# A third seven-product pair in the last step of both MLPs, totals added by accumulating transfers, main banks read out beside the last group

## The chip, the cores and the metric

The kernel runs on one core of one Trainium2 chip. The metric is the device time of one execution in microseconds (us); the time before is the median of three runs, 2081.15 us (2080.92 to 2085.08).

The core's engines are TensorE (PE in the profile, with its weight loads as PEld), VectorE (DVE), ScalarE (ACT), GpSimd (POOL) and SyncE (SP). SP issues the weight loads; POOL issues the transfers that add to their destination.

## The reference

Two layers over 256 tokens of width 2048. Layer 0 mixes with a gated short convolution, layer 1 with a stick-breaking attention; after each mixer comes a squared-ReLU MLP with a hidden width of 8192, and each sub-layer is added to the stream behind a norm. The change lies in the two MLPs only:

```python
def sq_relu_mlp(u, w_up, w_down):
    return jnp.square(jax.nn.relu(u @ w_up)) @ w_down

h = h + rmsnorm(sq_relu_mlp(u, mlp_w_up[i], mlp_w_down[i]), mlp_post_g[i])
```

## The kernel before

**Products.** Every fp32 operand is split into a high and a low part (`whi`, `wlo` for the weights), and a product is three matmuls: high by high, high by low, low by high. A weight chunk is 128 rows by 1024 columns. SP loads it into one of five buffers (`raw`, with the chunk's number behind it), ACT rounds it to `whi` (L184, or L233 in a seven), DVE subtracts to `wlo` (L195); seven buffers of each hold the parts. A `raw` buffer is given to the chunk five places later once both have read it, a `whi` and `wlo` buffer to the one seven places later once PE has used it.

**Eights and sevens.** A pair of chunks meets the two blocks of 128 tokens in eight products of 128 by 512 columns (24 matmuls, L1308 to L1310), or, by Winograd's scheme, in seven (21 matmuls). A seven costs DVE four differences of 128x512 over the weights (L225) and 3.5 splits in place of two, and four small differences of 128x128 over the hidden rows (L1170, with splits by L1127). Its parts carry the letters a, b, t, u and take four of the seven buffers. It needs four main banks in PSUM and four more for the products 1, 5, 6 and 7; combinations of these are then added to the main results.

**Steps.** Each MLP runs through eight steps e. In step e PE builds the hidden rows of step e+1 (`up`) and multiplies those of step e by the down weights. The last step (e = 7) has no `up`. It runs four pairs m = 0 to 3 onto the left half of the output, which close the main banks and the banks of the products 1, 5, 6 and 7, and then a last group of eight chunks onto the right half. Before the change m = 0 and 1 were sevens, m = 2 and 3 eights. Chunks 368 to 375 are the pairs and 376 to 383 the last group in MLP 0; 752 to 759 and 760 to 767 in MLP 1.

**The last group.** It reuses the banks of the products 1, 5, 6, 7 (numbers 6, 7, 0, 1), into which ACT first copies the partial results (L1375, `acc<-mg`). The blocks first take turns by units (a chunk against a block, both halves; 12 `acc` matmuls a chunk), over two chunks in MLP 1 and four in MLP 0; then each quarter of the output runs through its remaining chunks alone, so that its norm (`post`: a square on ACT, L687 or L779, and a gain on DVE, L567) starts as early as it can. Quarters are (block, column); (0,0) to (1,1) are the left half, (0,2) to (1,3) the right.

**Order.** PE keeps the order of the program. ACT and DVE are ordered when the kernel is built, by a scheduler with priorities (`tc.high_priority`), and while a norm runs, by a manual order that follows the program's own clock (`at(delay, fn)`, `spent(us)`). Each engine works through its rows in order, so a row that waits holds up all behind it. In MLP 0 the norm is followed by the groups for keys and values (`KeyNorms`, chunks from 384, banks 4, 5 for block 0 and 6, 7 for block 1), whose first operand is the transposed new residual; in MLP 1 by the output (`OutNorms`).

Of the kernel before, what the change touches and what calls it, by code (L numbers as in the profile page):

```python
# [14 lines left out]
P = 128  # L15
# [90 lines left out]
def trunk(ctx, tc, x, xT, vecs, rows, ws, out):  # L106
# [201 lines left out]
    def at(delay, fn):  # L308
        heappush(due, (clock["us"] + delay, clock["seq"], fn))
        clock["seq"] += 1  # L310

    def spent(us):
        clock["us"] += us
        while due and due[0][0] <= clock["us"]:
            heappop(due)[2]()
# [150 lines left out]
                self.add_total(r, ps, (b, c))  # L466
            self.then(b, c, r if not self.early else ps[:], r)

    def run(groups, enter=False, leave=None):

        units = [(gr, i) for gr in groups for i in range(gr.n)]
        first, last = EDGE if enter else 0, len(units) - (leave.edge if leave else 0)
# [645 lines left out]
    def mlp(pool, i, before, after):  # L1118
# [10 lines left out]
        class Hidden:  # L1129


            def __init__(self, e):
                self.xs, self.sums = [None] * (NF // 4), {}
# [7 lines left out]
            def tile(self, n, ps, half):  # L1141
                if n % 2 == 0:
                    held[n] = pool.tile([P, 2, T], F32, tag="s", name="s", bufs=2)
                both = held[n - n % 2]
                s = both[:, n % 2, :]
                with tc.high_priority():
                    nc.vector.tensor_tensor(s, ps[:, :T], half[:], op=ALU.add)  # L1147
                nc.scalar.activation(s, s, AF.Relu)  # L1148
                nc.scalar.activation(s, s, AF.Square)
                if self.xs[n // 4] is None:  # L1150
                    self.xs[n // 4] = operand("hid4")
                if n - n % 2 in self.apart or n - n % 2 not in self.pairs:
                    split_tile(self.xs, n, s)
                if n % 2:
                    del held[n - 1]
                    if n - 1 in self.pairs:
                        self.sums[n - 1] = self.sums_of(n - 1, both)

            def sums_of(self, n, both):

                t = after.dump()
                s2, s3, s4 = (t[:, j * P : (j + 1) * P] for j in range(3))
                a11, a21, a12, a22 = (both[:, j // 2, j % 2 * P : (j % 2 + 1) * P] for j in range(4))
                apart = n in self.apart
                s1 = t[:, 3 * P :] if apart else a21
                for to, v, w, op in (
                    (s3, a11, a21, ALU.subtract), (s1, a21, a22, ALU.add),
                    (s2, s1, a11, ALU.subtract), (s4, a12, s2, ALU.subtract),
                ):
                    nc.vector.tensor_tensor(to, v, w, op=op)  # L1170
                if apart:
                    one = pool.tile([P, 2, P], F32R, tag="d", name="sums", bufs=2)
                    one = [one[:, j, :] for j in range(2)]
                    two_parts(one, s1)
# [7 lines left out]
                return [one] + [[m[:, j * P : (j + 1) * P] for m in more] for j in range(3)]  # L1182

        pss, adds = {}, []

# [59 lines left out]
                low(first, k, k, n)  # L1245
            finish(to, n)

        def add(j, b, c, ps, last=False):
            r = part[b][2 * j + c]
            with tc.high_priority():  # L1250
                if r is None:
# [1 line left out]
                    nc.scalar.activation(r, ps[:], AF.Copy)  # L1253
                else:
                    nc.vector.tensor_tensor(r, r, ps[:], op=ALU.add)
            if last:
                after.post(b, 2 * j + c, r, r, scale[b][:])

        def add_later(j, p1, p5, p6, p7):
            t = pool.tile([P, 4, 512], F32, tag="gpost", name="more", bufs=1)  # L1260
# [12 lines left out]
                (r[1, 1], t7), (r[0, 1], t6), (r[1, 0], t6), (r[1, 1], t6),  # L1273
            ))

        def add_now(j, p1, p5, p6, p7):
            w = pool.tile([P, 4, 512], F32, tag="gpre", name="more", bufs=1)
            t, u2, u3, u4 = (w[:, m, :] for m in range(4))
            nc.scalar.activation(t, p1[:], AF.Copy)
            nc.vector.tensor_tensor(u2, t, p6[:], op=ALU.add)  # L1280
            nc.vector.tensor_tensor(u3, u2, p7[:], op=ALU.add)
            nc.vector.tensor_tensor(u4, u2, p5[:], op=ALU.add)
            nc.vector.tensor_tensor(u2, u3, p5[:], op=ALU.add)
            rs = [part[b][2 * j + c] for b in range(NB) for c in range(2)]
            for r, v in zip(rs, (t, u4, u3, u2)):
                nc.vector.tensor_tensor(r, r, v, op=ALU.add)

        class Down:

# [22 lines left out]
            def pair(self, at, first, xs):  # L1312
# [1 line left out]
                seven = m in SEVEN[e][at[2]]  # L1314
                (self.seven if seven else self.eight)(at, first, xs, 2 * m)
                if at == self.range["fifth"][1]:
                    ps = [self.ps.pop(n) for n in (1, 5, 6, 7)]
                    self.combine = lambda: (add_now if at[0] == STEPS - 1 else add_later)(self.j, *ps)
                    if at != self.plan[-1]:
                        self.combine()  # L1320
                        self.combine = None
                if at == self.plan[-1]:
                    last = e == STEPS - 1
                    for b, c in sorted(self.ps):
                        add(self.j, b, c, self.ps.pop((b, c)), last)
                    if self.combine:
                        self.combine()
# [29 lines left out]
        for e in range(STEPS):  # L1357
            first = W["mlp", i, e + 1].base
            if e == STEPS - 1:
# [12 lines left out]
                for b in range(NB):  # L1372
                    for c in range(2):
                        ps = final.ps[b, c] = bank(LAST_BANKS[b][c], "acc")
                        nc.scalar.activation(ps[:], part[b][2 * j + c], AF.Copy)  # L1375
# [218 lines left out]
    run(groups, enter=True, leave=Late())  # L1594

    pool1, mix1 = held["pool1"], held["mix1"]
    mlp(pool1, 1, mix1, OutNorms(pool1, None))
# [84 lines left out]
```

## Time and profile before

| | |
|---|---|
| median of three runs | 2081.15 us |
| the profiled execution | 2081.61 us, with a span of 2079.8 us from first to last instruction |
| DVE busy 970 to 980, 990 to 1000, 1000 to 1010, 1010 to 1020 us | 9.95, 9.67, 7.94, 5.20 of 10 us |
| DVE busy 2030 to 2040, 2040 to 2050, 2050 to 2060 us | 9.95, 9.97, 8.11 of 10 us |
| share of the 16 DMA engines, 940 to 950 and 2040 to 2050 us | 0.91, 0.78 |
| PE's granted clock | 0.999 of full speed |

The last step of MLP 0 lies between 974.5 and 1017 us, that of MLP 1 between 2029 and 2072 us. The second follows the first at a distance of 1054.54 us (the pair m = 2 starts at 984.05 and at 2038.59). Rows of a timeline begin with start and duration in us. A PE row's duration is longer than the distance to the next row, since matmuls overlap: distances between starts are what counts there, and on DVE and ACT too.

### The profile page before, as it was taken

How to read it: one execution, taken by the hardware profiler on the slowest of the kernel's cores; microseconds unless marked ns; L12 is line 12 of the kernel's file. 1: busy time of each engine (PE TensorE's matmuls, PEld its weight loads, DVE VectorE, ACT ScalarE, POOL GpSimd, SP SyncE). 2: the span in 40 equal slices, each digit the busy share in tenths (PEclk: the TensorE clock that was granted, in tenths of full speed). 3: DMA queues.
4: the chain of work that ended last, by engine and by line, in shares of the span. 5: the costliest groups of instructions: out<-in, count | busy, mean ns of one | idle time of the engine just before them, and what ended most of it. 6: DMA issues, size and time to landing. Idle time of an engine off the chain costs nothing.

```text
span 2079.8 us, 29874 instructions
## 1 busy us (share of the span) xinstructions
PE 2071.7 (100%) x10535; PEld 1768.0 (85%) x10535; DVE 1945.0 (94%) x2916; ACT 1497.8 (72%) x2199; POOL 117.7 (6%) x147
## 2 busy tenths in 40 slices
PE   9999999999999999999999999999999999999998
PEld 8888888888888888888888888889888888888886
DVE  8999999999999999999897777888999999999997
ACT  7766656777777777777588888657777777777774
POOL 0000000010100101101000000000001010010010
PEclk9999999999999999999999999999999999999999
DMA  8666585577877878778565555655687697787784
GB/s 306 214 196 218 184 274 176 197 233 226 241 219 240 237 220 253 221 229 251 192 193 183 160 162 183 200 194 173 210 246 235 210 249 224 229 248 220 232 243 164
DMA packets 133717, 451.45 MB, mean 217 GB/s; under 512 B 15008, under 2 KB 15520, under 8 KB 133056
## 3 DMA queue, kind: packets, MB, share of 16 engines
q1 hardware_dynamic: 113472, 406.68, 60.5%
q0 software_dynamic: 19952, 42.61, 10.0%
q8 instruction: 82, 1.34, 0.3%
q14 instruction: 67, 0.55, 0.1%
q10 hardware_dynamic: 144, 0.26, 0.0%
HBM read 415.42 MB, written 2.10 MB: 201 GB/s over the span
## 4 chain that ended last, share of the span: by engine, by line
PE 97%; DVE 1%; DMA 1%; issue 0%; ACT 0%; SPq 0%; DVEq 0%; ACTq 0%
PE up L1195 21%; PE up L1202 12%; PE acc L893 7%; PE acc L346 7%; PE acc L348 7%; PE acc L347 7%; PE more L1309 5%; PE more L1308 5%; PE more L1310 5%; PE acc L1308 4%; PE acc L1309 4%; PE acc L1310 4%; PE lead L893 1%; PE up L1197 1%; PE tr L278 1%; PE more L1028 1%
## 5 line engine op out<-in xcount | busy, mean ns | idle before, releaser
L195 DVE TENSOR_TENSOR wlo<-raw,whi 128x1024 fp32r<-128x1024 f32 (+1 forms) x398 | 474.4, 1201 | 13.4 <-ACT whi L184 12.9
L184 ACT ACTIVATE whi<-raw 128x1024 fp32r<-128x1024 f32 (+1 forms) x398 | 409.2, 1044 | 104.9 <-PE up L1195 39.2
L1195 PE MATMUL up<-u,whi 128*128 128x512 f32 x1952 | 465.0, 389 | 0.0
L1195 PEld LDWEIGHTS up<-u,whi 128*128 128x128 f32 x1952 | 365.0, 188 | 74.7
L1202 PEld LDWEIGHTS up<-u,wlo 128*128 128x128 f32 x2048 | 263.6, 191 | 10.3
L1202 PE MATMUL up<-u,wlo 128*128 128x256 f32 x2048 | 268.0, 283 | 0.0
L225 DVE TENSOR_TENSOR sums<-raw,sums 128x512 f32<-128x512 f32 x264 | 180.1, 682 | 0.8
L1208 ACT ACTIVATE half<-up 128x256 f32<-128x256 f32 x128 | 49.1, 385 | 133.7 <-PE up L1202 131.2
L346 PE MATMUL acc<-whi,u 128*128 128x512 f32 x360 | 143.6, 399 | 0.0
L348 PE MATMUL acc<-whi,u 128*128 128x512 f32 x360 | 140.5, 390 | 0.0
L1215 POOL DMA_DIRECT2D mg<-more x108 | 93.6, 867 | 826.1 <-ACT more L1270 382.0
L347 PE MATMUL acc<-wlo,u 128*128 128x512 f32 x360 | 140.3, 390 | 0.0
L197 DVE SCALAR_TENSOR_TENSOR wlo<-raw,gv,whi 128x512 fp32r<-128x512 f32 (+1 forms) x148 | 122.9, 860 | 14.7 <-ACT whi L184 14.2
L184 ACT ACTIVATE whi<-raw,gv 128x512 fp32r<-128x512 f32 (+1 forms) x148 | 113.2, 807 | 27.1 <-PE acc L348 12.1
L893 PE MATMUL acc<-u,whi 128*128 128x512 f32 x416 | 97.8, 389 | 0.0
L225 DVE TENSOR_TENSOR sums<-raw,raw 128x512 f32<-128x512 f32 x132 | 90.1, 682 | 4.8 <-DMA raw<-w_mlp 4.4
L893 PEld LDWEIGHTS acc<-u,whi 128*128 128x128 f32 x416 | 77.8, 188 | 15.9
L225 DVE TENSOR_TENSOR sums<-raw 128x512 f32<-128x512 f32 x132 | 90.0, 682 | 1.1 <-DMA raw<-w_mlp 1.0
L348 PEld LDWEIGHTS acc<-whi,u 128*128 128x128 f32 x360 | 67.6, 188 | 14.7
L346 PEld LDWEIGHTS acc<-whi,u 128*128 128x128 f32 x360 | 67.7, 188 | 12.8 <-DVE mg L567 0.4
L347 PEld LDWEIGHTS acc<-wlo,u 128*128 128x128 f32 x360 | 67.8, 188 | 12.5
L1148 ACT ACTIVATE s<-s 128x256 f32<-128x256 f32 x128 | 51.8, 408 | 5.1 <-DVE s L1147 4.4
(7192 smaller groups left out, 4770.1 us busy)
## 6 DMA issues: line engine op xcount, KB each, us to landing
raw<-w_mlp SPq DMA_DIRECT2D x512, 512.0 KB, 4.6
raw<-w_in SPq DMA_DIRECT2D x94, 512.0 KB, 4.4
mg<-more POOLq DMA_DIRECT2D x108, 256.0 KB, 6.3
raw<-w_out SPq DMA_DIRECT2D x32, 512.0 KB, 4.8
raw<-w_v SPq DMA_DIRECT2D x32, 512.0 KB, 4.5
raw<-w_wo SPq DMA_DIRECT2D x32, 512.0 KB, 4.2
raw<-w_k SPq DMA_DIRECT2D x24, 512.0 KB, 4.5
raw<-w_q SPq DMA_DIRECT2D x24, 512.0 KB, 3.7
```

The costliest lines, as they stand in the source:

```text
L184: rounded = nc.scalar.activation(hi[:, at], raw[i][:, at], AF.Copy, scale=1.0 if gain is None else gain)
L195: nc.vector.tensor_tensor(lo[:, at], t[:, at], hi[:, at].bitcast(F32), op=ALU.subtract)
L225: nc.vector.tensor_tensor(t, x, y, op=ALU.subtract)
L346: nc.tensor.matmul(ps[:], xh, hi[:, a], start=first, stop=False, skip_group_check=skip)
L347: nc.tensor.matmul(ps[:], xh, lo[:, a], start=False, stop=False, skip_group_check=skip)
L348: self.done = nc.tensor.matmul(ps[:], xl, hi[:, a], start=False, stop=last, skip_group_check=skip)
L893: nc.tensor.matmul(ps[:, :cols], w, xs[:, :cols], start=k == 0 and part == parts[0], stop=k == KD - 1 and part == parts[1], skip_group_che ...
L1195: nc.tensor.matmul(ps, weight(0, first, m), x, start=k == 0, stop=False)
L1202: nc.tensor.matmul(pss[n][:, :T], weight(1, first, m), x, start=False, stop=k == KD - 1)
L1308: nc.tensor.matmul(self.ps[key][:], xh, hi, start=first, stop=False)
L1309: nc.tensor.matmul(self.ps[key][:], xh, lo, start=False, stop=False)
L1310: self.done = nc.tensor.matmul(self.ps[key][:], xl, hi, start=False, stop=last)
```

## The change

The third pair, m = 2, becomes a seven (`SEVEN`). Its hidden rows also need the four differences; the split of their first one is put off until the last hidden tile is done (`behind`). The totals of the products 1, 5, 6, 7 close with m = 2; four DVE adds form the combinations, and four transfers on POOL add them to the left half's partial results, where four DVE adds did so before. The main banks, read out by DVE right behind m = 3 before, are read out by `add_last`, put off by 5.4, 6.8, 8.1 and 9.5 us of the program's clock, beside the last group. The last group takes the banks 6, 0, 1, 7 in place of 6, 7, 0, 1, and begins with two units of block 0 and then two of block 1, where the blocks took turns.

```diff
-LAST_BANKS = [[6, 7], [0, 1]]
+LAST_BANKS = [[6, 0], [1, 7]]
-SEVEN = [((0, 1, 2, 3),) * 2] * (STEPS - 1) + [((0, 1), ())]
+SEVEN = [((0, 1, 2, 3),) * 2] * (STEPS - 1) + [((0, 1, 2), ())]
+LAST_ADDS = (5.4, 6.8, 8.1, 9.5)
...
+                if n == NF - 1 and self.behind:
+                    self.behind()
...
+                    if n < NF // 2:
+                        one = split_first("d")
+                    else:
+                        one, self.behind = None, lambda: self.sums[n].insert(0, split_first("half"))
...
-            if last:
-                after.post(b, 2 * j + c, r, r, scale[b][:])
+        def add_last(j, b, c, ps):
+            r = part[b][2 * j + c]
+            nc.vector.tensor_tensor(r, r, ps[:], op=ALU.add)
+            after.post(b, 2 * j + c, r, r, scale[b][:])
...
-        def add_now(j, p1, p5, p6, p7):
+        def totals(j, p1, p5, p6, p7):
             w = pool.tile([P, 4, 512], F32, tag="gpre", name="more", bufs=1)
             t, u2, u3, u4 = (w[:, m, :] for m in range(4))
             nc.scalar.activation(t, p1[:], AF.Copy)
...
-            rs = [part[b][2 * j + c] for b in range(NB) for c in range(2)]
-            for r, v in zip(rs, (t, u4, u3, u2)):
-                nc.vector.tensor_tensor(r, r, v, op=ALU.add)
+            for n, v in enumerate((t, u4, u3, u2)):
+                nc.gpsimd.dma_start(part[n // 2][2 * j + n % 2], v, accum_op=ALU.add)
...
+                        if e == STEPS - 1:
+                            defer(LAST_ADDS[n], lambda what=(self.j, b, c, ps): add_last(*what))
...
-                        nc.scalar.activation(ps[:], part[b][2 * j + c], AF.Copy)
+                        with tc.high_priority():
+                            nc.scalar.activation(ps[:], part[b][2 * j + c], AF.Copy)
                 final.begun = True
-                run([final], leave=after)
+                run([final], enter=2, leave=after)
```

DVE's rows at the end of MLP 1, before, from the totals to the split of the last chunk (`more` are the totals, `mg` the partial results of the left half, `acc` and the last `more` the main banks):

```order
L1283 TENSOR_TENSOR more_20530<-more_20530,more_20133 128x512
L1286 TENSOR_TENSOR mg_15830<-mg_15830,more_20530 128x512
...
L195 TENSOR_TENSOR wlo759_20541<-raw759_20440,whi759_20540 128x1024
...
L1255 TENSOR_TENSOR mg_15828<-mg_15828,acc_20125 128x512
L195 TENSOR_TENSOR wlo762_20584<-raw762_20507,whi762_20583 128x1024
...
L195 TENSOR_TENSOR wlo764_20644<-raw764_20550,whi764_20643 128x1024
L567 SCALAR_TENSOR_TENSOR mg_15832<-mg_15832,hs_20466,gpost_20468 128x512
L195 TENSOR_TENSOR wlo765_20660<-raw765_20556,whi765_20659 128x1024
L567 SCALAR_TENSOR_TENSOR mg_15835<-mg_15835,hs_20466,gpost_20468 128x512
L195 TENSOR_TENSOR wlo766_20678<-raw766_20587,whi766_20677 128x1024
L195 TENSOR_TENSOR wlo767_20685<-raw767_20593,whi767_20684 128x1024
```

The same place in the changed kernel:

```order
L1296 TENSOR_TENSOR more_20608<-more_20608,more_20158 128x512
L196 TENSOR_TENSOR wlo760_20582<-raw760_20523,whi760_20581 128x1024
...
L1299 TENSOR_TENSOR more_20608<-more_20608,more_20154 128x512
L196 TENSOR_TENSOR wlo762_20625<-raw762_20552,whi762_20624 128x1024
L196 TENSOR_TENSOR wlo763_20631<-raw763_20579,whi763_20630 128x1024
...
L196 TENSOR_TENSOR wlo765_20680<-raw765_20622,whi765_20679 128x1024
L1271 TENSOR_TENSOR mg_15849<-mg_15849,acc_20146 128x512
L196 TENSOR_TENSOR wlo766_20708<-raw766_20628,whi766_20707 128x1024
L570 SCALAR_TENSOR_TENSOR mg_15849<-mg_15849,hs_20496,gpost_20500 128x512
L196 TENSOR_TENSOR wlo767_20715<-raw767_20634,whi767_20714 128x1024
L1271 TENSOR_TENSOR mg_15851<-mg_15851,acc_20150 128x512
```

Three of the four main adds and their gains have moved behind `wlo767`; one add and one gain stand right ahead of `wlo766` and `wlo767`. On ACT the squares of the left half now follow `whi767`.

DVE's rows at the end of MLP 0, before, from the split of the last chunk to the first new residual (`h`), for which PE's first transposes wait (384 to 386 are chunks of the values):

```order
L195 TENSOR_TENSOR wlo383_10352<-raw383_10247,whi383_10351 128x1024
L197 SCALAR_TENSOR_TENSOR wlo384_10370<-raw384_10301,gv_83,whi384_10369 128x1024
L197 SCALAR_TENSOR_TENSOR wlo385_10376<-raw385_10319,gv_83,whi385_10375 128x1024
L197 SCALAR_TENSOR_TENSOR wlo386_10382<-raw386_10337,gv_83,whi386_10381 128x1024
L567 SCALAR_TENSOR_TENSOR mg_4640<-acc_10289,hs_10118,gpost_10122 128x512
...
L516 RECIPROCAL rstd_10422<-rstd_10422 128x1
L635 SCALAR_TENSOR_TENSOR h_2583<-mg_5482,rstd_10422,h_2583 128x512
```

And in the changed kernel:

```order
L1271 TENSOR_TENSOR mg_5486<-mg_5486,acc_9799 128x512
L196 TENSOR_TENSOR wlo383_10369<-raw383_10267,whi383_10368 128x1024
L570 SCALAR_TENSOR_TENSOR mg_5484<-mg_5484,hs_10129,gpost_10133 128x512
L1271 TENSOR_TENSOR mg_5489<-mg_5489,more_10287 128x512
L570 SCALAR_TENSOR_TENSOR mg_5486<-mg_5486,hs_10131,gpost_10133 128x512
L198 SCALAR_TENSOR_TENSOR wlo384_10391<-raw384_10306,gv_83,whi384_10390 128x1024
L570 SCALAR_TENSOR_TENSOR mg_5489<-mg_5489,hs_10131,gpost_10133 128x512
L198 SCALAR_TENSOR_TENSOR wlo385_10397<-raw385_10318,gv_83,whi385_10396 128x1024
L198 SCALAR_TENSOR_TENSOR wlo386_10403<-raw386_10346,gv_83,whi386_10402 128x1024
L570 SCALAR_TENSOR_TENSOR mg_4640<-acc_10294,hs_10129,gpost_10133 128x512
...
L519 RECIPROCAL rstd_10443<-rstd_10443 128x1
L638 SCALAR_TENSOR_TENSOR h_2583<-mg_5482,rstd_10443,h_2583 128x512
```

A main add and three gains of the left half now lie between `wlo383` and the first residual, where the splits of 383 to 386 followed each other directly.

More of the change, by code (lines that the diff above doesn't have):

```diff
@@ L467, in add_and_evict, with run @@
             self.then(b, c, r if not self.early else ps[:], r)
-    def run(groups, enter=False, leave=None):
+    def run(groups, enter=0, leave=None):
         units = [(gr, i) for gr in groups for i in range(gr.n)]
-        first, last = EDGE if enter else 0, len(units) - (leave.edge if leave else 0)
+        first, last = enter, len(units) - (leave.edge if leave else 0)
         for b in range(NB):
@@ L1132, in __init__ @@
             def __init__(self, e):
-                self.xs, self.sums = [None] * (NF // 4), {}
+                self.xs, self.sums, self.behind = [None] * (NF // 4), {}, None
                 first, second = SEVEN[e]
@@ L1171, in sums_of, with split_first @@
                 if apart:
-                    one = pool.tile([P, 2, P], F32R, tag="d", name="sums", bufs=2)
-                    one = [one[:, j, :] for j in range(2)]
-                    two_parts(one, s1)
+                    def split_first(tag):
+                        one = pool.tile([P, 2, P], F32R, tag=tag, name="sums", bufs=2)
+                        one = [one[:, j, :] for j in range(2)]
+                        two_parts(one, s1)
+                        return one
+                    if n < NF // 2:
+                        one = split_first("d")
+                    else:
+                        one, self.behind = None, lambda: self.sums[n].insert(0, split_first("half"))
                 else:
@@ L1181, in sums_of @@
                 two_parts(more, t[:, : 3 * P])
-                return [one] + [[m[:, j * P : (j + 1) * P] for m in more] for j in range(3)]
+                return [one][: one is not None] + [[m[:, j * P : (j + 1) * P] for m in more] for j in range(3)]
         pss, adds = {}, []
@@ L1246, in whole_up, with add @@
             finish(to, n)
-        def add(j, b, c, ps, last=False):
+        def add(j, b, c, ps):
             r = part[b][2 * j + c]
@@ L1279, in add_now @@
             nc.scalar.activation(t, p1[:], AF.Copy)
[L1280 to L1283, printed above, removed]
-            rs = [part[b][2 * j + c] for b in range(NB) for c in range(2)]
-            for r, v in zip(rs, (t, u4, u3, u2)):
-                nc.vector.tensor_tensor(r, r, v, op=ALU.add)
+            with tc.high_priority():
+                nc.vector.tensor_tensor(u2, t, p6[:], op=ALU.add)
+                nc.vector.tensor_tensor(u3, u2, p7[:], op=ALU.add)
+                nc.vector.tensor_tensor(u4, u2, p5[:], op=ALU.add)
+                nc.vector.tensor_tensor(u2, u3, p5[:], op=ALU.add)
+            for n, v in enumerate((t, u4, u3, u2)):
+                nc.gpsimd.dma_start(part[n // 2][2 * j + n % 2], v, accum_op=ALU.add)
         class Down:
@@ L1316, in pair @@
                 if at == self.range["fifth"][1]:
[L1317 to L1321, printed above, removed]
-                if at == self.plan[-1]:
[L1323 to L1327, printed above, removed]
+                    more = [self.ps.pop(n) for n in (1, 5, 6, 7)]
+                    if e == STEPS - 1:
+                        totals(self.j, *more)
+                if at == self.plan[-1]:
+                    for n, (b, c) in enumerate(sorted(self.ps)):
+                        ps = self.ps.pop((b, c))
+                        if e == STEPS - 1:
+                            defer(LAST_ADDS[n], lambda what=(self.j, b, c, ps): add_last(*what))
+                        else:
+                            add(self.j, b, c, ps)
+                    if e < STEPS - 1:
+                        add_later(self.j, *more)
             def seven(self, at, first, xs, n):
@@ L1374, in mlp @@
                         ps = final.ps[b, c] = bank(LAST_BANKS[b][c], "acc")
-                        nc.scalar.activation(ps[:], part[b][2 * j + c], AF.Copy)
+                        with tc.high_priority():
+                            nc.scalar.activation(ps[:], part[b][2 * j + c], AF.Copy)
                 final.begun = True
-                run([final], leave=after)
+                run([final], enter=2, leave=after)
                 break
@@ L1593, in trunk @@
     groups += project(W["wo"], o, lambda: held["mix1"], WO_MIXED)
-    run(groups, enter=True, leave=Late())
+    run(groups, enter=EDGE, leave=Late())
     pool1, mix1 = held["pool1"], held["mix1"]
```

1 line of the change is left out of this document (added).

## The prediction

> **What bounds the kernel now.** I read the page's busy times and chain first, then the two places of the change in the timelines of PE and DVE, then the chain near the end.
>
> ```profile
> PE 2071.7 (100%) x10535; PEld 1768.0 (85%) x10535; DVE 1945.0 (94%) x2916; ACT 1497.8 (72%) x2199; POOL 117.7 (6%) x147
> PE 97%; DVE 1%; DMA 1%; issue 0%; ACT 0%; SPq 0%; DVEq 0%; ACTq 0%
> ```
>
> PE is busy for all but 8 us of the span, and the chain is PE for 97%: a matmul less is time saved, and any other work is free as long as PE isn't made to wait. DVE, at 94%, is the engine that could make it wait. How PE moves is read from the distance of rows:
>
> ```profile
> 984.05 0.39 PE L1308 MATMUL acc<-whi,hid 128*128 128x512 f32 x1
> ...
> 994.93 0.39 PE L346 MATMUL acc<-whi,hid 128*128 128x512 f32 x1
> 1014.66 0.60 PE L278 MATMUL tr<-ident,h 128*128 128x128 f32 x4
> ```
>
> From 984.05 to 994.93 lie the pairs m = 2 and 3, 48 matmuls without a gap: 10.88 / 48 = **0.227 us each**. PE reaches the first transposes 19.73 us after the last group's start.
>
> PE's small stalls near the change:
>
> ```profile
> 1023.55 0.39 PE L348 MATMUL acc<-whi,u 128*128 128x512 f32 x1
> 1023.96 0.50 PE L346 MATMUL acc<-whi,u 128*128 128x512 f32 x1
> 2058.32 0.39 PE L346 MATMUL acc<-whi,hid 128*128 128x512 f32 x1
> 2058.86 0.50 PE L347 MATMUL acc<-wlo,hid 128*128 128x512 f32 x1
> 2044.94 5.36 DMA raw<-w_mlp
> 2056.53 2.28 DVE wlo L195 x2
> 2058.86 0.50 PE acc L347
> ```
>
> The distances 0.41 and 0.54 are 0.18 and 0.31 too long. The last three rows are from the chain in order of time: the end of MLP 1 already goes through a weight load, DVE's last two splits (766, 767), and then PE. There DVE has nothing in hand.
>
> **The matmuls removed.** A seven has 21 where an eight has 24: 3 x 0.227 = 0.68 us, in each MLP. **-1.36 us.**
>
> **DVE and ACT at the third pair.** All of the pair's new DVE work lies beside PE's work; what counts is when each part is ready.
>
> ```profile
> 969.06 1.23 DVE L195 TENSOR_TENSOR wlo368b<-raw,whi368b 128x1024 fp32r<-128x1024 f32 x1 [0.30 <-PE up L1202]
> 978.67 1.23 DVE L195 TENSOR_TENSOR wlo370u<-sums,whi370u 128x1024 fp32r<-128x1024 f32 x1
> 979.81 3.49 DVE L195 TENSOR_TENSOR wlo<-raw,whi 128x1024 fp32r<-128x1024 f32 x3
> 983.22 0.68 DVE L1280 TENSOR_TENSOR more<-more 128x512 f32<-128x512 f32 x1
> 983.82 0.68 DVE L1286 TENSOR_TENSOR mg<-mg,more 128x512 f32<-128x512 f32 x1
> ```
>
> A full split takes 3.41 / 3 = 1.14 us, a 512-column add, difference or split 0.60. The hidden rows' four differences and two small splits:
>
> ```profile
> 914.39 0.28 DVE L1170 TENSOR_TENSOR sq<-s,sq 128x128 f32<-128x128 f32 x1
> 914.59 1.22 DVE L195 TENSOR_TENSOR wlo<-raw,whi 128x1024 fp32r<-128x1024 f32 x1
> 916.33 0.55 DVE L1127 TENSOR_TENSOR sums<-sq,sums 128x384 fp32r<-128x384 f32 x1
> 916.80 0.68 DVE L225 TENSOR_TENSOR sums<-raw,raw 128x512 f32<-128x512 f32 x1
> ```
>
> That is 5 x 0.20 + 0.47 = 1.47 us, less the 0.30 that DVE waited at 969.06: `wlo370u` ends at 979.81 + 1.17 = 981.0. The seven follows: part a at 981.6, three differences and b at 984.55, the fourth and t at 986.3, u at 987.4. PE needs b at its 5th matmul (984.96), t at the 11th (986.32), u at the 17th (987.68). Ready within 0.0 to 0.4 us of need, with nothing to spare: 0 to 0.3 us of stall, and I take 0.1 in each MLP, since two of three are early. **+0.2 us.** PE then starts the last group at 984.05 + 0.1 + 45 x 0.227 = 994.4.
>
> DVE goes on: 374 at 988.55, 375 at 989.7, the totals between 376 and 377, the last one at 994.5, 378 at 995.6. The totals free the banks in the order 6, 0, 1, 7 in which the last group takes them.
>
> ```profile
> 983.75 1.10 ACT L1375 ACTIVATE acc<-mg 128x512 f32<-128x512 f32 x2
> ```
>
> A copy into a bank takes 0.55 us. The one into bank 7 is due at 994.4 + 15 x 0.227 = 997.8 and stands on ACT behind `whi380`, which is loaded once 375 is split: 989.8, a load of 5.0 to 6.3 us (below), 0.95 and 0.55 us make 996.3 to 997.6. I cost it at nothing; a load 0.2 us slower than that would use the cover up.
>
> **The end of MLP 1.** (In MLP 0's times; add 1054.54.) Chunk 383's load can start when 378 is split, at 995.7. Loads of this part take, by the rows of `raw` between 2036 and 2056 us:
>
> ```profile
> DMA to landing us min/median/max: 5.0/5.4/6.3
> 996.41 0.71 ACT L687 ACTIVATE sq<-mg,hs 128x512 f32<-128x512 f32 x1
> 997.03 0.19 ACT L687 ACTIVATION_READ_ACCUMULATOR sq<-mg,hs 128x1 f32 x1
> 997.12 1.05 ACT L184 ACTIVATE whi<-raw 128x1024 fp32r<-128x1024 f32 x1
> 998.07 0.71 ACT L687 ACTIVATE sq<-mg,hs 128x512 f32<-128x512 f32 x1
> ```
>
> So it lands at 1000.7 to 1002.0; `whi` takes 0.95, then ACT squares (0,0), 0.9 with its accumulator's reading, then DVE does that quarter's gain (0.66), which stands ahead of the split, then `wlo` (1.14): 1004.3 to 1005.7. PE needs it after 4 units, 5 chunks of a quarter and one matmul: 994.4 + 40 x 0.227 = 1003.5. A stall of 0.8 to 2.2 us, for which I take 1.6 and subtract the 0.31 that goes: **+1.3 us.** The chain gets a load, a `whi` and a square in a row where DVE's adds had been.
>
> **The end of MLP 0.** Four chunks per block come first there, so 383 isn't due until 994.4 + 58 x 0.227 = 1007.6, and it is ready at 1005.5 to 1006.9 (two more adds stand ahead of it). But DVE's queue goes on to the norm:
>
> ```profile
> 1007.20 1.28 DVE L197 SCALAR_TENSOR_TENSOR wlo<-raw,gv,whi 128x1024 fp32r<-128x1024 f32 x1 [0.94 <-ACT whi L184]
> 1009.61 0.75 DVE L567 SCALAR_TENSOR_TENSOR mg<-acc,hs,gpost 128x512 f32<-128x512 f32 x1 [1.12 <-ACT sq L687]
> 1012.33 0.29 ACT L515 ACTIVATE rstd<-ss,bias 128x1 f32<-128x1 f32 x1
> 1012.65 0.16 DVE L516 RECIPROCAL rstd<-rstd 128x1 f32<-128x1 f32 x1 [1.85 <-ACT rstd L515]
> 1012.85 0.75 DVE L635 SCALAR_TENSOR_TENSOR h<-mg,rstd,h 128x512 f32<-128x512 f32 x1
> ```
>
> Before, the first residual ended at 1013.60, 1.06 us ahead of PE's transposes (1014.66). Now three gains, an add and three splits of 1.2 us (6.2 us in all) bring the gain of (0,2) to 1011.7 to 1013.1, and gain, bias, root, reciprocal and residual (0.66 + 0.55 + 0.35 + 0.2 + 0.75 = 2.5) to 1014.2 to 1015.6. PE is there at 994.4 + 19.7 = 1014.1. A stall of 0.1 to 1.5 us: **+0.9 us.**
>
> **Bank 7.** The stall of 0.18 at 1023.96 is the values' second bank of block 1, number 7, waiting for the gain that reads it:
>
> ```profile
> 1023.16 1.40 DVE L567 SCALAR_TENSOR_TENSOR mg<-acc,hs,gpost 128x512 f32<-128x512 f32 x2
> PEld acc L346 <- DVE mg L567: 0.4, 1, 0.4
> ```
>
> Two gains stand there, of (0,3) and then (1,3). Bank 7 held (0,3) and now holds (1,3): it comes free one gain later, **+0.66 us**, and nothing hides it, since this DVE row is set by the transposes that PE has just done.
>
> **The transfers.** Their issues occupy POOL alone; the totals leave between 989.8 and 995.
>
> ```profile
> L1215 POOL DMA_DIRECT2D mg<-more x108: 847/867/892, 444.4 to 2029.5; - x108
> DMA to landing us min/median/max: 3.3/6.3/8.1
> ```
>
> Even at 8.1 us the first is there by 998.7, and its add stands behind 381, near 999.5; the last is there near 1004, its add near 1007. Cost nothing, unless they delay weight loads (below).
>
> **The sum.** -1.36 + 0.2 + 1.3 + 0.9 + 0.66 = **+1.7 us**. The profiled execution took 2081.61 us, 1.8 more than its span; the changed kernel would take 2083.3 beside it. The median is 0.46 lower, so I predict **2082.9 us**. With all low ends it is -1.36 - 0.31 + 0.66 = -1.0; with all high ones -1.36 + 0.6 + 1.9 + 1.5 + 0.66 = +3.3.
>
> **Rival 1: the covers hold.** If the loads land early and ACT's and DVE's rows interleave well, only the matmuls and the two old stalls go: -1.36 - 0.31 - 0.18 = -1.85, **2079.3 us**. For it: before, PE waited only 0.5 us over both MLPs' ends, with DVE as full; DVE has 2.06 us of idle time ahead of 1009.61 that my walk spends. Against it: three waits on this path with less than 0.4 us to spare each, and bank 7.
>
> **Rival 2: the transfers delay the weight loads, and it is slower.**
>
> ```profile
> DMA packets 133717, 451.45 MB, mean 217 GB/s; under 512 B 15008, under 2 KB 15520, under 8 KB 133056
> q1 hardware_dynamic: 554, 2.01, 61.6%
> q0 software_dynamic: 286, 0.52, 29.0%
> ```
>
> The last two rows are the queues between 940 and 950 us: two adding transfers took 29% of the 16 engines for 10 us, 1.45 us each, and 2.01 MB of weights (3.8 chunks) 61.6%, 1.6 us each. Between 988 and 1001, 12.6 us, the changed kernel wants seven chunks and four transfers, 17.0 us of the engines in MLP 0; in MLP 1, where five chunks are left, 13.8. So the last loads come up to 4.4 and 1.2 us late, and these fall on the two stalls above: 1.7 + 5.6 = +7.3, **2088.5 us**. It decides from some 2.5 us of lateness on. Against it: these loads are spread by the buffers that free them.
>
> [...]
>
> **How the numbers follow.** My forecast has 0.60, rival 1 0.26, rival 2 0.13, and 0.01 is left. 0.2% (4.2 us) is about what a measurement can tell from no change. Forecast and rival 1 lie within it, rival 2 mostly outside. Range 2079.0 to 2085.4: it takes in rival 1, with 0.3 us for the scatter between runs, and the high ends, and leaves most of rival 2 out.
>
> **What would show it.** In the changed profile: PE's rows 6 fewer; a gap of about 0.84 at the first matmul on `u` of the second half bank in MLP 0; a gap of about 1 us ahead of the first transposes; a gap of 1 to 2 us ahead of a low part in the last chunk of MLP 1. If PE has none of these gaps, rival 1 holds; if loads of the last chunks take over 7 us to land, rival 2. I'm wrong altogether if PE waits for something else, such as the copies into the banks.

## The result, and the profile after

| | before | changed |
|---|---|---|
| median of 6 runs | 2081.18 us | 2092.09 us |
| lowest to highest | 2080.55 to 2085.08 us | 2088.54 to 2093.48 us |
| span of the profiled execution | 2079.8 us | 2091.0 us |
| PE's last group begins, MLP 0 | 994.93 | 993.69 |
| last matmul of MLP 1's tail (`end<-mg,roots`) | 2074.10 | 2084.81 |

The ratio is 1.0047, with a 95% interval of 1.0034 to 1.006: the changed kernel is slower. Up to the last group of MLP 0 it is 1.2 us ahead; at the tail of MLP 1 it is 10.7 us behind, so 11.9 us are lost in between, in the last groups of the two MLPs and just behind them. The waits of PE in the changed kernel (waiting operation, what it waited for: us in all, times, longest):

```profile
PE acc L350 <- DVE wlo L196: 3.5, 3, 2.1
PE tr L279 <- DVE h L638: 2.7, 1, 2.7
...
PE acc L349 <- DVE mg L570: 0.7, 1, 0.7
PE acc L349 <- ACT whi L185: 0.5, 1, 0.5
```

The three rows left out (`end`, `warm` and `lead`) come to what they did before, and a last one of 0.2 us (the copy into bank 7) is not shown; these are new. All are waits for DVE or ACT, but these two waited in turn. ACT's timeline in the changed kernel, at the last chunks of MLP 0 and of MLP 1 (start, us, what; the idle time ahead of it, and what ended that):

```profile
995.84 1.06 ACT L185 ACTIVATE whi<-raw 128x1024 fp32r<-128x1024 f32 x1 [2.77 <-DMA raw<-w_mlp]
...
1000.49 1.06 ACT L185 ACTIVATE whi<-raw 128x1024 fp32r<-128x1024 f32 x1 [1.99 <-DMA raw<-w_mlp]
1003.14 1.06 ACT L185 ACTIVATE whi<-raw 128x1024 fp32r<-128x1024 f32 x1 [1.59 <-DMA raw<-w_mlp]
1004.11 0.71 ACT L690 ACTIVATE sq<-mg,hs 128x512 f32<-128x512 f32 x1
...
2063.39 1.06 ACT L185 ACTIVATE whi<-raw 128x1024 fp32r<-128x1024 f32 x1 [1.40 <-DMA raw<-w_mlp]
2064.35 0.71 ACT L782 ACTIVATE sq<-mg,hs 128x512 f32<-128x512 f32 x1
```

ACT, busy for 72% of the span, stands still for 1.4 to 2.8 us at a time until a weight load lands. Its squares stand behind that `whi`, DVE's gains behind the squares, DVE's next split behind the gains. The rows of DVE that follow the last two, ahead of PE's wait at 2067.12:

```profile
2065.18 0.75 DVE L570 SCALAR_TENSOR_TENSOR mg<-mg,hs,gpost 128x512 f32<-128x512 f32 x1 [1.93 <-ACT sq L782]
2065.85 1.22 DVE L196 TENSOR_TENSOR wlo<-raw,whi 128x1024 fp32r<-128x1024 f32 x1
```

The loads between 988 and 1000 us (size, median us to landing), beside the four transfers:

```profile
raw<-w_mlp SPq DMA_DIRECT2D x5, 512.0 KB, 6.9
raw<-w_v SPq DMA_DIRECT2D x3, 512.0 KB, 9.3
mg<-more POOLq DMA_DIRECT2D x4, 256.0 KB, 9.1
```

The transfers land late too, but that holds nothing up by itself: none of DVE's eight main adds, which need their sums, has idle time ahead of it (999.67 to 1009.03 and 2060.22 to 2072.82). PE itself, at the two long waits:

```profile
1014.56 0.39 PE L351 MATMUL acc<-whi,hid 128*128 128x512 f32 x1
1017.65 1.09 PE L279 MATMUL tr<-ident,h 128*128 128x128 f32 x4 [2.71 <-DVE h L638]
...
1018.97 0.63 PE L350 MATMUL acc<-wlo,hid 128*128 128x512 f32 x1
1019.40 0.63 PE L351 MATMUL acc<-whi,hid 128*128 128x512 f32 x1
...
2064.50 0.50 PE L349 MATMUL acc<-whi,hid 128*128 128x512 f32 x1 [0.46 <-ACT whi L185]
2067.12 0.79 PE L350 MATMUL acc<-wlo,hid 128*128 128x512 f32 x1 [2.12 <-DVE wlo L196]
```

The gaps are plain. The second loss is easily overlooked, since no wait is put down to it: the matmuls behind a gap stand 0.43 us apart (1018.97 to 1019.40) instead of 0.227, until 1021.10 in MLP 0, and in MLP 1 until 2072.41. Two windows of the changed kernel (busy us of PE, PEld, DVE, ACT, POOL with their counts, then the granted clock of PE, the DMA share, GB/s) show the clock; over the slow stretches alone (1017.65 to 1021.10 and 2067.12 to 2072.41) it is 0.51 and 0.50:

```profile
1015.00:1025.00 10.00, 7.35 (x27) 6.08 (x28) 6.21 (x16) 3.67 (x8) 0.00 (x0) 0.83 0.32 106
2060.00:2070.00 10.00, 6.66 (x21) 4.39 (x20) 5.96 (x8) 3.64 (x6) 0.00 (x0) 0.78 0.20 61
```

Before, the first of these windows had a clock of 1.00 and 49 matmuls:

```profile
1015.00:1025.00 10.00, 9.99 (x49) 7.93 (x48) 6.95 (x13) 4.90 (x9) 0.36 (x1) 1.00 0.19 52
```

### The profile page after: what moved, and what is told of

Same layout as the page of the kernel before. It is cut to its first block, busy times and chain, and to the rows that moved or that the text cites. A ratio compares the mean times of both kernels' runs of the same rounds, so it can differ in the third digit from the quotient of the medians.

```text
span 2091.0 us, 29902 instructions
## 1 busy us (share of the span) xinstructions
PE 2075.2 (99%) x10529; PEld 1769.8 (85%) x10529; DVE 1952.5 (93%) x2932; ACT 1502.0 (72%) x2207; POOL 124.7 (6%) x155
## 3 DMA queue, kind: packets, MB, share of 16 engines
q0 software_dynamic: 21104, 44.71, 10.5%
## 4 chain that ended last, share of the span: by engine, by line
PE 94%; DVE 3%; DMA 1%; issue 1%; ACT 1%; SPq 0%; DVEq 0%; ACTq 0%
PE up L1207 21%; PE up L1214 11%; PE acc L896 7%; PE acc L349 6%; PE acc L350 6%; PE acc L351 6%; PE more L1324 5%; PE more L1323 5%; PE more L1325 5%; PE acc L1323 4%; PE acc L1324 4%; PE acc L1325 4%; PE lead L896 1%; PE up L1209 1%; PE tr L279 1%; DVE sums L226 1%
## 5 line engine op out<-in xcount | busy, mean ns | idle before, releaser
L896 PEld LDWEIGHTS acc<-u,wlo 128*128 128x128 f32 x416 | 52.8, 191 | 1.6
```

The lines of the kernel that those rows point to most:

```text
L896: nc.tensor.matmul(ps[:, :cols], w, xs[:, :cols], start=k == 0 and part == parts[0], stop=k == KD - 1 and part == parts[1], skip_group_che ...
```

## The experiments

Theory **T**: the four adding transfers take the DMA engines just as the last weight loads run (between 988 and 1000 us the transfers' queue has 39.7% of the 16 engines, that of the loads 57.1%); the loads come late, and by way of `whi`, squares, gains and splits PE waits; and where it waits long (3.09 and 2.62 us from start to start, above), its clock is halved for some us afterwards (3.45 and 5.29). Rivals: **O**, that the new order on DVE and ACT is late by itself, and **B**, that the new banks and the group's new beginning are what costs. From e7 on the runs also look for a version that beats the kernel before.

| run | median us | ratio to before, 95% interval |
|---|---|---|
| changed kernel | 2092.09 | 1.0047 (1.0034 to 1.006) |
| e1: transfers left out | 2080.66 | 0.9999 (0.999 to 1.0008) |
| e2: DVE adds on the spot | 2083.28 | 1.001 (1.0001 to 1.002) |
| e3: third pair as eight | 2082.77 | 1.0008 (0.9998 to 1.0017) |
| e4: banks as before | 2090.40 | 1.0045 (1.0028 to 1.0061) |
| e5: idle matmuls, bank 4 | 2095.17 | 1.0067 (1.0052 to 1.0082) |
| e6: two transfers, two DVE adds | 2084.75 | 1.0017 (1.0007 to 1.0027) |
| e7: DVE adds at the read-out, banks reordered | 2082.82 | 1.0009 (0.9999 to 1.0018) |
| e8: as e7, banks of the change | 2083.11 | 1.0011 (1.0002 to 1.0021) |
| e9: idle matmuls, banks 4 and 3 | 2089.43 | 1.004 (1.0026 to 1.0053) |
| e10: as e7, second half read out later | 2083.95 | 1.0011 (1.0003 to 1.002) |
| e11: as e2, main banks read out at once | 2088.66 | 1.0036 (1.0023 to 1.005) |
| e12: as e7, times apart for each MLP | 2084.92 | 1.0019 (1.001 to 1.0028) |

### e1: the transfers left out

```diff
-            for n, v in enumerate((t, u4, u3, u2)):
-                nc.gpsimd.dma_start(part[n // 2][2 * j + n % 2], v, accum_op=ALU.add)
```

> The changed kernel with its four adding transfers of each MLP left out, so that the four totals are worked out and never added; all else as in the change. Theory T (the transfers take the DMA engines from the last weight loads; loads late, so ScalarE's high parts, its squares, VectorE's gains and low parts are late, TensorE waits, and after each long wait its clock is halved for some us): the last loads land in 5 to 7 us as before the change, the waits of 3.1 us ahead of the first transposes and of 1.3, 0.9 and 2.6 us in the last chunks of MLP 1 go, and with them the matmuls that stand 0.43 us apart; 2081 to 2084 us. Theory O (the order on VectorE and ScalarE is late by itself: sums of the third pair, totals at high priority, the later read-out of the main banks): 2090 to 2093 us, the waits stay. Theory B (the new bank order and the second group's entry by two chunks): stays within 1 us of 2092 too.

2080.66 us, 0.3 below the bounds of T: the whole loss goes. All of PE's waits in this run:

```profile
PE end L799 <- ACT roots L798: 1.4, 1, 1.4
PE warm L886 <- DVE ones L126: 1.1, 1, 1.1
PE acc L349 <- DVE mg L570: 0.7, 1, 0.7
```

The loads between 988 and 1000 us in this run, to be read against the same rows above:

```profile
raw<-w_mlp SPq DMA_DIRECT2D x5, 512.0 KB, 4.5
raw<-w_v SPq DMA_DIRECT2D x4, 512.0 KB, 5.7
```

They land 2.4 and 3.6 us sooner. ACT's waits for `whi380` to `whi383` of MLP 0 are 0.42, 0.17, 1.26 and 0.88 us here, against 2.77, 0, 1.99 and 1.59 in the changed kernel. The order on DVE and ACT, the banks and the entry are those of the change, so O and B don't explain the loss. This run also gives the account. Against it the changed kernel's `end<-mg,roots` is 12.46 us later (2084.81 against 2072.35), and the gaps, each less 0.23 for the matmul itself, add up to that. In MLP 0 they are 0.36 (the copy into bank 7), 0.75 (`wlo`, 1007.10 to 1008.08), 2.86 (first transposes) and 1.73 for the slow clock (the transposes 0.39, then six matmuls in 2.70 us instead of 1.36). In MLP 1 they are 1.03, 0.63 and 2.39 in the last two chunks of the first quarter, and 2.57 for the slow clock (5.29 us from 2067.12 to 2072.41, in which twelve matmuls would take 2.72). **8.0 us of waits, 4.3 us of slow clock**, 12.3 of 12.46.

### e2: DVE adds in place of the transfers

```diff
-                nc.gpsimd.dma_start(part[n // 2][2 * j + n % 2], v, accum_op=ALU.add)
+                r = part[n // 2][2 * j + n % 2]
+                nc.vector.tensor_tensor(r, r, v, op=ALU.add)
```

> The changed kernel with its adding transfers replaced by four VectorE adds at the same place in the program (four of some 0.6 us of VectorE in each MLP, no transfer); the result is the same. Theory T: loads land in 5 to 7 us; VectorE is given 2.5 us of work where it waited for ScalarE in the changed kernel, so 2082 to 2085 us. Theory O: VectorE is what is late, and 2.5 us more of it makes it worse: 2093 to 2097 us.

As T said, and against O: 2.5 us more DVE work in each MLP makes the kernel 8.8 us faster than the changed one. The loads land in 4.5 us (median, 5.7 at most, in both MLPs). What the adds cost by themselves is the difference to e1, 2.6 us, in small waits of PE:

```profile
PE acc L350 <- DVE wlo L196: 1.3, 3, 0.6
PE tr L279 <- DVE h L638: 0.8, 1, 0.8
```

### e3: the third pair as eight products

```diff
-SEVEN = [((0, 1, 2, 3),) * 2] * (STEPS - 1) + [((0, 1, 2), ())]
+SEVEN = [((0, 1, 2, 3),) * 2] * (STEPS - 1) + [((0, 1), ())]
```

> The changed kernel with the third pair of the last step as eight products again (24 matmuls instead of 21, no sums of it); totals still added by transfers, which now start a pair earlier, about 5 us. Theory T: four transfers meet loads all the same, but loads of weights that are needed 5 us later, and the last ones go free: between 2083 and 2090 us, and the landing of the loads right behind the transfers still 7 to 10 us. Theory O, if the sums of the third pair are what is late: 2083 to 2085 us, with the loads as in the changed kernel. Theory B: 2091 to 2094 us.

2082.77 us, 0.2 below the bounds of both T and O, with six matmuls (1.36 us) more than the changed kernel. By the time alone, O's sums could have been the cause. The loads decide. Their landing in this run, by the rows of `raw` between 984 and 1000 us:

```profile
DMA to landing us min/median/max: 5.7/9.4/10.9
```

The same between 2036 and 2056 us:

```profile
DMA to landing us min/median/max: 7.9/11.0/11.6
```

They are later than in the changed kernel beside its transfers (median 7.4 between 984 and 1000 us, and 7.1 between 2048 and 2056), and only one wait of 0.2 us comes of it. The transfers start a pair earlier, and the loads that they delay are needed later. So late loads don't harm by themselves; it matters **when** they come. That is in part argued, since this run also takes the third pair's sums off DVE.

### e4: the banks as before

```diff
-LAST_BANKS = [[6, 0], [1, 7]]
+LAST_BANKS = [[6, 7], [0, 1]]
```

> The changed kernel with the last group's banks as before the change (quarters (0,0), (0,1), (1,0), (1,1) in banks 6, 7, 0, 1). Theory T: only the wait at bank 7 (1.04 us at the first matmul of the next stage that uses it in MLP 0) goes, so 2090.5 to 2091.5 us, or no change that can be told if another wait comes there; the other waits stay. Theory B: 2082 to 2086 us.

2090.4 us: at the lower bound that was expected, but not for the reason given. The 0.7 us at bank 7 is gone, and two new waits came, both for the copy into the bank that the totals set free last. The first of PE's waits in this run:

```profile
PE acc L349 <- ACT acc L1392: 4.8, 2, 2.7
```

And PE's timeline at one of the two:

```profile
994.58 0.39 PE L351 MATMUL acc<-whi,hid 128*128 128x512 f32 x1
997.08 0.50 PE L349 MATMUL acc<-whi,hid 128*128 128x512 f32 x1 [2.11 <-ACT acc L1392]
...
998.13 0.63 PE L350 MATMUL acc<-wlo,hid 128*128 128x512 f32 x1
998.55 0.63 PE L351 MATMUL acc<-whi,hid 128*128 128x512 f32 x1
```

They stand at the group's beginning, and seem to give the loads the time that they lack: no wait for a low part or for the residual is left on the list. The clock falls here too (0.91 between 990 and 1000 us), 1 us behind the gap, for 3.4 us.

### e5 and e9: does the halved clock cost by itself?

Idle matmuls into a free bank, ahead of the operations that waited:

```diff
+    def fill(n, number=4):
+        ps = bank(number, "fill")
+        for _ in range(n):
+            nc.tensor.matmul(ps[:], *near["x"], start=True, stop=True, skip_group_check=True)
...
         def between(self, what):
 
+            fill(10)
             self.enter(0, 0)
...
                 final.begun = True
+                if i == 1:
+                    fills.update({(final, 0, 0, 6, 1): 4, (final, 0, 0, 7, 0): 2, (final, 0, 0, 7, 1): 8})
```

> The changed kernel with idle matmuls, whose results nobody reads, put on TensorE where it waited: ten into bank 4 ahead of the first transposes of MLP 0, and four, two and eight in the last two chunks of the first quarter in MLP 1, each of operands that are there already. They take the place of waiting (10 and 14 by 0.227 us are 2.3 and 3.2 us), so the work behind the waits starts when it did; transfers and loads stay as late as in the changed kernel. Theory T with the clock as a part of its own (a wait of 2 to 3 us halves the clock for 3.4 to 5.3 us afterwards, which costs about half of that): the matmuls after the waits stand 0.23 us apart instead of 0.43, granted clock 1.00 there, and the time falls by 1.6 us (MLP 0) and 2.5 us (MLP 1), to 2087 to 2089 us. If the matmuls are far apart for another reason (operands late, the weights' port, transfers in SBUF): no gain, 2091 to 2094 us.

Slower than the changed kernel, by a mistake of the experiment: in MLP 1 bank 4 isn't read out yet when the idle matmuls come to it.

```profile
PE fill L331 <- DVE mg L1284: 4.8, 1, 4.8
```

The run says nothing of MLP 1. In MLP 0 the matmuls behind the transposes stood 0.23 us apart. With bank 3 in MLP 1 (the edit is the bank's number in those three calls):

> The idle matmuls once more, those of MLP 1 now in bank 3, which is read out before TensorE comes to them (bank 4, which they had, is not, and TensorE waited 4.84 us for it); MLP 0 as before. Clock theory: in MLP 0 again matmuls 0.23 us apart behind the first transposes; in MLP 1 the same behind the fills, no wait over 1.3 us and granted clock 1.00; the time falls by the lost half clock, to 2087 to 2089 us from the changed kernel's 2092. If the clock is not what costs: 2091 to 2094 us.

PE's timeline in e9, at the first transposes:

```profile
1015.15 2.44 PE L331 MATMUL fill<-whi,hid 128*128 128x512 f32 x10
1017.43 0.60 PE L279 MATMUL tr<-ident,h 128*128 128x128 f32 x4
...
1018.10 0.40 PE L362 MATMUL acc<-wlo,hid 128*128 128x512 f32 x1
1018.34 0.40 PE L363 MATMUL acc<-whi,hid 128*128 128x512 f32 x1
```

The same two windows as above, now of e9:

```profile
1015.00:1025.00 10.00, 10.00 (x50) 8.28 (x49) 6.01 (x15) 3.87 (x9) 0.00 (x0) 1.00 0.37 108
2060.00:2070.00 10.00, 9.73 (x42) 7.25 (x41) 6.11 (x8) 4.17 (x9) 0.00 (x0) 1.00 0.04 9
```

The transposes start at nearly the same time (1017.43 against 1017.65), the loads are as late (median 7.6 us between 984 and 1000 us, against 7.4), and the clock stays at 1.00. The profiled span is 4.5 us shorter than that of the changed kernel, where the account had 4.3 for the clock; the medians differ by 2.7, a little less than the 3.1 to 5.1 of the expectation, and the changed kernel's own runs lie 5 us apart. They point the same way: the one of 2088.54 us has a granted clock of 0.999 over the span, that of 2090.45 has 0.998, and the four of 2091.39 to 2093.48 have 0.997. That the clock is a cost of its own, and that PE's idleness brings it on, is shown; its size is 2.7 to 4.5 us.

### e6: half the transfers

```diff
-            for n, v in enumerate((t, u4, u3, u2)):
-                nc.gpsimd.dma_start(part[n // 2][2 * j + n % 2], v, accum_op=ALU.add)
+            for n, v in enumerate((t, u4)):
+                nc.gpsimd.dma_start(part[0][2 * j + n], v, accum_op=ALU.add)
+            totals_of.update({(1, 0): u3, (1, 1): u2})
...
             r = part[b][2 * j + c]
+            if b:
+                nc.vector.tensor_tensor(r, r, totals_of.pop((b, c)), op=ALU.add)
             nc.vector.tensor_tensor(r, r, ps[:], op=ALU.add)
```

> The changed kernel with two of the four transfers in each MLP ((0,0) and (0,1)); the totals of (1,0) and (1,1) are added by VectorE at the later read-out of their main banks. The result is the same. Theory T: half the bytes beside the last loads, so loads about half as late (median 5.5 to 6.5 us of those behind them, none over 8.5), waits under 1.5 us each, the clock not halved: 2082 to 2086 us. If it is not the bytes but that any transfer of this kind stands in the queue or that the totals wait: 2088 to 2092 us.

2084.75 us. The loads between 984 and 1000 us land in 4.7 us (median) without transfers, in 6.1 with two and in 7.4 with four: the lateness grows with the bytes. In the profiled run no clock was lost in the two last groups: behind the waits of 2.00 and 1.67 us from start to start (1014.19 to 1016.19 and 2059.80 to 2061.47) the matmuls soon stand 0.23 us apart. Two of this run's waits, the first a little over the 1.5 us expected:

```profile
PE tr L279 <- DVE h L638: 1.6, 1, 1.6
PE acc L350 <- DVE wlo L196: 1.3, 1, 1.3
```

### e7, e8: DVE adds at the later read-out, and the banks

```diff
-            for n, v in enumerate((t, u4, u3, u2)):
-                nc.gpsimd.dma_start(part[n // 2][2 * j + n % 2], v, accum_op=ALU.add)
+            totals_of.update({(n // 2, n % 2): v for n, v in enumerate((t, u4, u3, u2))})
...
+            nc.vector.tensor_tensor(r, r, totals_of.pop((b, c)), op=ALU.add)
             nc.vector.tensor_tensor(r, r, ps[:], op=ALU.add)
...
-DOWN_BANKS = {(0, 0): 3, (0, 1): 4, (1, 0): 5, (1, 1): UP_BANK, 1: 6, 5: 7, 6: 0, 7: 1}
-LAST_BANKS = [[6, 0], [1, 7]]
+DOWN_BANKS = {(0, 0): 3, (0, 1): 4, (1, 0): 5, (1, 1): UP_BANK, 1: 6, 5: 1, 6: 7, 7: 0}
+LAST_BANKS = [[6, 7], [0, 1]]
```

e8 has the first two edits and the banks of the change.

> A version of the change: no transfer; each total is added by VectorE just ahead of the later read-out of its main bank (four more of 0.6 us, spread over the first half of the last group instead of on the spot); and the extra products p5, p6, p7 in banks 1, 7, 0 so that bank 7 holds quarter (0,1) of the last group as before the change and is set free in the order in which the group takes the banks. The result is the same. Theory T: loads land as without transfers (median under 5 us); the 0.57 us waits for the low parts just behind the totals go, what is left is 2.5 us of VectorE where it has slack, and the 0.67 us wait at bank 7 in MLP 0 goes: 2079.5 to 2082 us. If VectorE's order there leaves no slack: 2082 to 2085 us.

> As the version with VectorE adds at the later read-out, but with the banks as in the change (bank 7 holds quarter (1,3)). Bank theory (the next stage's first use of bank 7 waits for the gain that VectorE makes last): the wait of some 0.65 us at the first matmul on the second half's bank in MLP 0 is there and is the whole difference, 0.5 to 0.8 us above the other version.

In e8 the wait at bank 7 stands as in the changed kernel. PE's timeline there:

```profile
1024.76 0.39 PE L351 MATMUL acc<-whi,u 128*128 128x512 f32 x1
1025.81 0.50 PE L349 MATMUL acc<-whi,u 128*128 128x512 f32 x1 [0.66 <-DVE mg L570]
```

In e7 the same matmul comes 0.38 us behind the one ahead of it instead of 1.05; so the banks can come free in the order in which the group takes them without this wait:

```profile
1024.84 0.40 PE L351 MATMUL acc<-whi,u 128*128 128x512 f32 x1
1025.22 0.50 PE L349 MATMUL acc<-whi,u 128*128 128x512 f32 x1
```

Of the 0.67 only 0.29 us is left in the medians (0.24 without e8's longest run, of 2335.15 us), less than expected and within the scatter of the runs; in the profiles e7's first transposes come 2.44 us behind the matmul ahead of them, e8's 2.16. The time of e7 is 0.8 us above the bounds of T and within those for no slack on DVE: the first transposes now wait for the residual, 2.0 us in MLP 0, and the end waits 2.1 instead of 1.4 us in MLP 1.

### e10, e12: moving the rest of DVE's work

```diff
-LAST_ADDS = (5.4, 6.8, 8.1, 9.5)
+LAST_ADDS = (5.4, 6.8, 14.7, 16.1)
```

in e10, and in e12 `((5.4, 6.8, 16.4, 17.7), (5.4, 6.8, 7.4, 8.1))`, one row for each MLP.

> The version with VectorE adds at the later read-out and the banks in the order in which they come free, with the two quarters of the second 128 rows, (1,0) and (1,1), read out later still, behind the first half's root (14.7 and 16.1 us behind the last pair instead of 8.1 and 9.5). Theory T says that without transfers only VectorE's order is left: the first residual of MLP 0, which the first transposes wait 2.0 us for, stands behind those two adds, read-outs and gains (2 by 0.68 and 0.75 us and two adds of 0.6); moved behind it, the wait goes or falls under 0.8 us, and the time is 2080 to 2081.5 us, about the kernel before. If that wait is set by something else (a late low part, the root): 2082 to 2083.5 us as before this edit.

> The version with VectorE adds at the later read-out and the banks in the order in which they come free, with the read-out's times set apart for the two MLPs: in MLP 0 the second half's two quarters 16.4 and 17.7 us behind the last pair, so behind the first residual; in MLP 1, where the end waited 3.9 us instead of 2.1 when they came late, 7.4 and 8.1 us (before: 8.1 and 9.5). Theory T with VectorE's order as all that is left: no wait over 0.3 us ahead of the first transposes of MLP 0 (2.0 us before), the wait at the end 1.4 to 2.1 us, 2080.0 to 2081.7 us, within 0.2% of the kernel before. If the wait only moves to the second half's residual or gains: 2082 to 2083.5 us.

Both are above all the bounds given. In e10 the wait that was aimed at falls from 2.0 to 0.7 us, and the end pays for it. PE's waits in e10:

```profile
PE end L799 <- ACT roots L798: 3.9, 1, 3.9
...
PE tr L279 <- DVE h L638: 0.7, 1, 0.7
```

In e12 the wait for the residual is gone; but the second half's squares now stand on ACT ahead of the read-out of the transposes, and wait there for DVE's adds. ACT's timeline in e12:

```profile
1017.50 0.72 ACT L690 ACTIVATE sq<-mg,hs 128x512 f32<-128x512 f32 x1 [2.21 <-DVE mg L1272]
...
1018.22 0.57 ACT L301 ACTIVATE u<-tr 128x512 fp32r<-128x512 f32 x1
```

And PE, which waits for that last row:

```profile
1018.85 0.50 PE L349 MATMUL acc<-whi,u 128*128 128x512 f32 x1 [1.98 <-ACT u L301]
```

Behind this wait too (2.38 us from start to start) the clock was halved: the matmuls stand 0.43 us apart between 1020.48 and 1023.04. No version beats the kernel before. Even e1, in which the totals aren't added at all, is only 0.4 us below it, and a bank order without the wait is worth 0.3 to 0.7 us more: by these figures some 1 us was to be gained here.

### e11: the main banks read out at once

```diff
-LAST_ADDS = (5.4, 6.8, 8.1, 9.5)
+LAST_ADDS = (0, 0, 0, 0)
```

on top of e2's edit.

> The version with VectorE adds on the spot in place of the transfers, with the four main banks read out at once behind the last pair instead of 5.4 to 9.5 us later: this undoes the later read-out alone. If the later read-out is worth something: four adds and four gains (4 by 0.68 and 0.75 us, 5.7 us of VectorE) stand ahead of the low parts of the next chunks, and TensorE waits for low parts early in the last group by 1 to 4 us in each MLP: 2085 to 2091 us against 2083.3. If it is worth nothing: 2082.5 to 2084 us.

5.4 us slower than e2: the later read-out is worth something, where the totals are added on DVE. In MLP 0 there is one wait, of 0.6 us; the long ones came in the middle of MLP 1's last group rather than at its beginning, and the clock fell behind them (matmuls 0.43 us apart). The second of the two, in e11's timeline (the first was 1.81 us from start to start, 2057.97 to 2059.78):

```profile
2060.36 0.39 PE L349 MATMUL acc<-whi,hid 128*128 128x512 f32 x1
2062.91 0.79 PE L350 MATMUL acc<-wlo,hid 128*128 128x512 f32 x1 [2.16 <-DVE wlo L196]
2063.50 0.63 PE L351 MATMUL acc<-whi,hid 128*128 128x512 f32 x1
```

## Why the prediction was wrong

The predicted 2082.9 us is 9.2 below the measured 2092.1, which lies outside the range. Point by point:

- **The transfers ("cost nothing, unless they delay weight loads").** This is the step that failed. The mechanism of rival 2 was the right one, and it had 0.13. Its working already had the numbers: seven chunks and four transfers want 17.0 us of the engines in 12.6. What was wrong is the argument against it, that the loads "are spread by the buffers that free them". They are; but the transfers aren't, all four leave within 4.9 us (988.96 to 993.82), and the loads that meet them are the last ones, with nothing behind them in which the lateness could be made up. The landing times of 5.0 to 6.3 us, on which the terms for both MLPs' ends rest, came from a stretch without such transfers, and were used as if the change left them alone. The medians of e1 and the changed kernel differ by 2.7 us (4.7 and 7.4), by an estimate nearly what two transfers take of the engines (2.9 us, by the 1.45 us each of the prediction's working); no run shows in what turn the packets of loads and transfers went. The sign that the prediction named for rival 2, loads of over 7 us, came: between 984 and 1000 us they took 7.4 us in the median and 10.5 at most.
- **Rival 2's price** (2088.5 us) was 3.6 us too low. What it lacked is the clock: the working took each matmul at 0.227 us whatever stood ahead of it. With 2.7 to 4.5 us for that, it would have been 2091 to 2093. That its waits fit so well in all (8.3 us by its working, 8.0 measured) is in part luck: it had 5.3 us of them in MLP 0 and 2.8 in MLP 1, and 4.0 and 4.1 were measured.
- **The end of MLP 1 (+1.3) and of MLP 0 (+0.9).** With the loads on time both are nothing: in e1 there is no wait at either place. The loads then land in 4.3 to 4.7 us (median), not 5.0 to 6.3, as in the kernel before in MLP 0 (4.4 between 984 and 1000 us); and the walk on DVE was too slow at the third pair (`wlo372u` ends at 986.5, where it had 987.4). So these terms were right only as places where lateness would show, and too large without transfers.
- **The third pair (+0.2):** no wait was found there, in e1 or in the changed kernel. Nothing instead of 0.2.
- **Bank 7 (+0.66):** right, in mechanism and size: a wait of 0.67 us in e1, while in e7, with another bank order, the distance is 0.38 us, near the 0.41 before.
- **The copy into a bank behind `whi380`, cost nothing with 0.2 us of cover:** the cover was used up, by 0.36 us in the changed kernel (996.86 to 997.45), as the load came late. In e1 it held.
- **The matmuls removed (-1.36):** right by count; six matmuls fewer on the page. With the two other terms that e1 bears out, bank 7's +0.66 and the old wait of 0.31 us that goes, the sum is -1.0; e1's tail comes 1.75 us earlier than that of the kernel before (2072.35 against 2074.10), and its median is 0.4 lower, with an interval from -2.1 to +1.7 us.

Of rival 1 it can be said that it holds once the transfers cost nothing, apart from bank 7: e1 is its test. What isn't settled is how the clock decides. In the profiled runs, ahead of MLP 1's output, waits of 2.38, 2.50, 2.55, 2.62, 3.08, 3.09 and 5.23 us (from start to start) were followed by half clock, waits of 2.00, 2.16 and 2.44 us were not. One kernel seems to go both ways: e8's runs of 2082.55 to 2083.16 us have a granted clock of 0.999, those of 2084.62 to 2085.25 have 0.998; at which wait they differ isn't known.

## What to carry to other kernels

Bulk transfers that are moved off an engine are not free where the loads that share the DMA engines with them are needed soon (here four transfers beside them made the loads land in 7.4 us instead of 4.7 in the median); add up the engines' time from their start to the last load's need, and move the transfers ahead of that or leave the work on the engine. In a kernel in which TensorE is hardly ever idle, price a wait of some 2.4 us or more with what may follow it: here 1.6 (e4, eight matmuls in 3.41 us) to 2.7 us (e11, 13 in 5.69) lost to slow matmuls. And an engine's in-order queue carries one late load on to everything behind it (here ACT stood still for 1.40 us ahead of its last `whi` in MLP 1, DVE for 1.93 us behind it, and PE for 2.12), so look at what stands behind the instruction that waits for the load, and not at the engine's busy share.

## What was not expected of the hardware

Behind most waits of some 2.4 us and more, from start to start, the granted clock fell to half (0.51 and 0.50 over the changed kernel's two slow stretches): matmuls 0.43 us apart instead of 0.227, for 3.4 us (1017.65 to 1021.10, and twice in e4), 5.3 us (2067.12 to 2072.41) or 5.7 us (e11, 2062.91 to 2068.60), also when the gap was over before it began (e4: gap ends at 997.08, first slow matmul at 998.13). What decides whether the clock falls, and for how long, is not shown: gaps of 2.38 to 3.09 us were enough in the changed kernel, e4, e11 and e12, yet 2.44 us passed without loss in e7. Two windows show this difference (columns as in the section on the result, with the granted clock third from the end), first e7's behind its 2.44 us (1013.46 to 1015.90):

```profile
1014.00:1024.00 10.00, 8.10 (x40) 6.79 (x41) 6.04 (x15) 4.38 (x10) 0.00 (x0) 1.00 0.34 106
```

and e12's behind its 2.38 us (1016.47 to 1018.85):

```profile
1015.00:1025.00 10.00, 7.85 (x27) 5.63 (x26) 7.21 (x13) 4.26 (x11) 0.00 (x0) 0.83 0.00 1
```
